# A row softmax on one core: exponentials in a register loop, broadcasting multiplications, one transfer queue

## The chip, the cores and the metric

The kernel runs on one core of a Trainium2 chip. Four of the core's engines matter here: VectorE (DVE in the profile), ScalarE (ACT), GpSimd (POOL) and SyncE (SP). SP computes nothing; it issues transfers. Transfers between the memory off the chip (DRAM in the names, HBM in the profile) and the core's own memory run on 16 DMA engines. They are issued from an engine's instruction queue: a transfer issued by SP goes into SP's data queue (q1 in the profile), one issued by ScalarE into ScalarE's (q10). Engines run on their own and meet at semaphores.

The metric is the device time of one execution in microseconds (us); less is better. The time before is 161.78 us, the median of three runs (161.41 to 161.79).

## What is computed

```python
def reference(x):                      # x: 16 x 1024 x 512, float32
    x_max = np.max(x, axis=-1, keepdims=True)
    exp_x = np.exp(x - x_max)
    return exp_x / np.sum(exp_x, axis=-1, keepdims=True)
```

These are 16,384 rows of 512 numbers. Each row takes a maximum, an exponential of every element less that maximum, the sum of the exponentials, and a multiplication by the sum's reciprocal. 33.55 MB go in and 33.55 MB come out.

## The kernel before

The rows are cut into eight chunks (`CHUNKS`). A chunk gives each of the 128 partitions 16 rows (`CHUNK`), 4.19 MB in all, and is one load (L71) and one store (L74). Its work is done in two groups of eight rows per partition (`GROUP`), so there are 16 groups. The core's memory has places for six chunks (`PLACES`, the tile `held`); results are written over the inputs. So six loads can be issued at once, and loads 6 and 7 go into the places of chunks 0 and 1 once those are stored. `LOAD_AFTER` puts them behind the stores 0 and 1 in the program.

One group takes these steps:

- `rowmax` (L88): one VectorE reduction over 8 x 512 elements of each partition gives eight negated maxima (`shift`).
- `exps` (L93): eight ScalarE instructions of 512 elements each. Each takes one maximum as bias and also accumulates the sum of its row (`sums`). In the profile each shows as an ACTIVATE and a read of the accumulator.
- `scale` (L104, L106): one VectorE reciprocal of the eight sums, then eight multiplications, each of one row by one number per partition.

VectorE does the maximum of group g and then the scaling of group g-1, so that ScalarE has a group to work on meanwhile. All loads are issued from SP's queue and all stores from ScalarE's. A store stands in ScalarE's instruction stream between exponentials; `STORE_BEHIND` says how many groups late. Tile, the framework, keeps the order in which the program is written and adds the semaphores. `loads_at_the_head` moves SP's first load in front of the barrier at the start of the program. The instructions of all loops are written out one by one: the loops in the source are Python's.

Of the kernel before, what the change touches and what calls it, by code (L numbers as in the profile page):

```python
# [1 line left out]

# [4 lines left out]

F32 = mybir.dt.float32
EXP = mybir.ActivationFunctionType.Exp
AX = mybir.AxisListType.X  # L10


CHUNK = 16
CHUNKS = 8
PLACES = 6
GROUP = 8

STORE_BEHIND = [1, 1, 1, 1, 0, 0, 0, 0]

LOAD_AFTER = {0: 6, 1: 7}  # L20


AT_HEAD = {mybir.EngineType.SP: 1}

def loads_at_the_head(nc):

    main, body = nc.main_func.blocks[0], nc.main_func.blocks[1]
    for engine, count in AT_HEAD.items():  # L30
        loads = [
            i
            for i in body.instructions
            if i.engine == engine and type(i).__name__ == "InstDMACopy"
        ][:count]
        barrier = next(
            n
            for n, i in enumerate(main.instructions)
            if i.engine == engine and type(i).__name__ == "InstDrain"
        )  # L40
        for load in loads:
            body.instructions.remove(load)
        main.instructions[barrier:barrier] = loads


@with_exitstack
def kernel(
    ctx: ExitStack,
    tc: tile.TileContext,
    x: bass.AP,  # L50
    out: bass.AP,
):
    nc = tc.nc
    nc.at_finalize(loads_at_the_head)
    P = nc.NUM_PARTITIONS

    x_rows = x.flatten_outer_dims().rearrange("(c p r) d -> c p r d", p=P, r=CHUNK)
    out_rows = out.flatten_outer_dims().rearrange("(c p r) d -> c p r d", p=P, r=CHUNK)
    n, _, _, d = x_rows.shape
    assert n == CHUNKS  # L60

    data = ctx.enter_context(tc.tile_pool(name="data", bufs=1))
    stats = ctx.enter_context(tc.tile_pool(name="stats", bufs=6))
    held = data.tile([P, PLACES * CHUNK, d], F32, name="held")

    def place(k):
        at = (k % PLACES) * CHUNK
        return held[:, at : at + CHUNK, :]

    def load(k):  # L70
        nc.sync.dma_start(out=place(k), in_=x_rows[k])  # L71

    def store(k):
        nc.scalar.dma_start(out=out_rows[k], in_=place(k))  # L74
        if k in LOAD_AFTER:
            load(LOAD_AFTER[k])

    per = CHUNK // GROUP
    groups = CHUNKS * per
    shift, sums = [None] * groups, [None] * groups  # L80

    def rows(g):
        at = (g % per) * GROUP
        return place(g // per)[:, at : at + GROUP, :]

    def rowmax(g):
        shift[g] = stats.tile([P, GROUP], F32, name="shift", tag="shift")
        nc.vector.reduce_max(out=shift[g], in_=rows(g), axis=AX, negate=True)  # L88

    def exps(g):  # L90
        sums[g] = stats.tile([P, GROUP], F32, name="sums", tag="sums")
        for r in range(GROUP):
            nc.scalar.activation(  # L93
                out=rows(g)[:, r, :],
                in_=rows(g)[:, r, :],
                func=EXP,
                bias=shift[g][:, r : r + 1],
                scale=1.0,
                accum_out=sums[g][:, r : r + 1],
            )  # L100

    def scale(g):
        recip = stats.tile([P, GROUP], F32, name="recip", tag="recip")
        nc.vector.reciprocal(out=recip, in_=sums[g])  # L104
        for r in range(GROUP):
            nc.vector.tensor_scalar_mul(  # L106
                out=rows(g)[:, r, :],
                in0=rows(g)[:, r, :],
                scalar1=recip[:, r : r + 1],
            )  # L110

    with tc.manual_schedule():
        for k in range(PLACES):
            load(k)
        stored = 0
        for g in range(groups):
            rowmax(g)
            exps(g)
            if g:
                scale(g - 1)  # L120
            if stored < CHUNKS and g > (stored + 1) * per - 1 + STORE_BEHIND[stored]:
                store(stored)
                stored += 1
        scale(groups - 1)
        while stored < CHUNKS:
            store(stored)
            stored += 1


# [1 line left out]
_INS = ['x']  # L131
_OUTS = [((16, 1024, 512), 'float32')]


# [23 lines left out]
```

## Time and profile before

| | |
|---|---|
| median of three runs | 161.78 us |
| the profiled execution | 161.69 us |
| its span, first to last instruction | 159.9 us |
| VectorE busy | 123.5 us, 77% |
| ScalarE busy | 93.2 us, 58% |
| GpSimd busy | 0.2 us |
| moved | 67.13 MB, mean 420 GB/s |
| a load, issue to landing (median) | 35.4 us |
| a store, issue to landing (median) | 28.4 us |

The profile comes from one execution. The span leaves out 1.8 us of the execution's time. Busy time of an engine counts its computing instructions; issuing a transfer is not counted. The DMA share is the mean busy share of the 16 DMA engines. A queue marked "q" behind an engine's name (SPq, ACTq) is the engine's instruction stream itself, where transfers are issued. A group of instructions is given by line, engine, operation, output <- input, shape and count, then its busy time, the mean of one in ns, and the idle time of the engine just before it with what ended that.

### The profile page before, as it was taken

What the parts mean: (1) busy time and instruction counts of PE and PEld (TensorE: products, weight loads), DVE (VectorE), ACT (ScalarE), POOL (GpSimd) and SP (SyncE); (2) the same over time, 40 slices, a digit from 0 to 9 for tenths busy, and PEclk for the clock granted to TensorE, in tenths of its full rate; (3) what the DMA queues carried; (4) which work ended last, traced back from release to release, by engine and by line L of the source; (5) the groups of instructions that cost most, each with busy time, mean ns of one, the idle gap of its engine ahead of it and who ended that gap; (6) DMA issues with size and microseconds to landing.
All of it is one profiled execution on the core that took longest, in us unless ns stands there. A gap on an engine that the chain in (4) does not pass through costs nothing.

```text
span 159.9 us, 496 instructions
## 1 busy us (share of the span) xinstructions
DVE 123.5 (77%) x160; ACT 93.2 (58%) x257; POOL 0.2 (0%) x4
## 2 busy tenths in 40 slices
DVE  0008969999999999999999999999999997620000
ACT  0003799495959585867777685959594959300000
POOL 0000000000000000000000000000000000000000
DMA  8999999999999999999999999999999999999993
GB/s 270 459 443 402 451 459 402 426 469 410 402 393 393 500 412 402 467 434 410 426 459 410 418 484 404 402 500 410 402 426 484 393 410 500 402 402 500 410 402 148
DMA packets 2307, 67.13 MB, mean 420 GB/s; under 512 B 256, under 2 KB 256, under 8 KB 256
## 3 DMA queue, kind: packets, MB, share of 16 engines
q1 hardware_dynamic: 1152, 33.55, 49.5%
q10 hardware_dynamic: 1152, 33.55, 48.6%
q14 instruction: 3, 0.02, 0.0%
HBM read 33.55 MB, written 33.55 MB: 420 GB/s over the span
## 4 chain that ended last, share of the span: by engine, by line
DMA 48%; DVE 32%; ACT 8%; issue 1%; DVEq 0%; SPq 0%; ACTq 0%
DMA held<-in_x_dram 30%; DVE shift L88 19%; DMA out_dram<-held 18%; DVE held L106 12%; ACT held L93 8%; DVE recip L104 1%; DVEq L153 0%; SPq L71 0%; ACTq L93 0%
## 5 line engine op out<-in xcount | busy, mean ns | idle before, releaser
L93 ACT ACTIVATE held<-held,shift 128x512 f32<-128x512 f32 x128 | 90.5, 708 | 31.5 <-DVE shift L88 21.3
L88 DVE TENSOR_REDUCE shift<-held 128x8 f32<-128x4096 f32 x16 | 70.5, 4415 | 12.7 <-DMA held<-in_x_dram 12.7
L106 DVE TENSOR_SCALAR held<-held,recip 128x512 f32<-128x512 f32 x128 | 52.1, 482 | 0.6
L93 ACT ACTIVATION_READ_ACCUMULATOR held<-held,shift 128x1 f32 x128 | 23.9, 187 | 0.0
L93 ACT ACT_TABLE_LOAD x1 | 1.3, 1283 | 12.6 <-DMA held<-in_x_dram 12.6
L104 DVE RECIPROCAL recip<-sums 128x8 f32<-128x8 f32 x16 | 3.1, 196 | 4.0 <-ACT held L93 4.0
L142 POOL MEMSET const-bfloat16-1.0<- 128x1 bf16 x1 | 0.1, 101 | 0.0
L142 POOL MEMSET const-uint8-127<- 128x1 uint8 x1 | 0.1, 101 | 0.0
L142 POOL MEMSET const-float32-0.0<- 128x1 f32 x1 | 0.1, 98 | 0.2 <-issue 0.2
L142 POOL MEMSET const-float32-1.0<- 128x1 f32 x1 | 0.1, 98 | 0.0
## 6 DMA issues: line engine op xcount, KB each, us to landing
held<-in_x_dram SPq DMA_DIRECT2D x8, 4096.0 KB, 35.4
out_dram<-held ACTq DMA_DIRECT2D x8, 4096.0 KB, 28.4
```

The costliest lines, as they stand in the source:

```text
L88: nc.vector.reduce_max(out=shift[g], in_=rows(g), axis=AX, negate=True)
L93: nc.scalar.activation(out=rows(g)[:, r, :], in_=rows(g)[:, r, :], func=EXP, bias=shift[g][:, r : r + 1], scale=1.0, accum_out=sums[g][:, ...
L104: nc.vector.reciprocal(out=recip, in_=sums[g])
L106: nc.vector.tensor_scalar_mul(out=rows(g)[:, r, :], in0=rows(g)[:, r, :], scalar1=recip[:, r : r + 1],)
L142: nc = _bacc.Bacc("TRN2", target_bir_lowering=False, num_devices=1)
```

## The change

The kernel no longer uses Tile's pools and semaphores for most of its work, but its own semaphores inside sections that Tile treats as one piece (`tile_critical`).

- **Transfers.** There are nine loads and nine stores of one or two groups (`SIZES`); group 0 has a buffer of its own (`first`), the fifteen others go round a ring of eleven groups (`ring`). All are issued by SP, in a fixed order: loads 0 to 6, then `ORDER`, then store 0. SP waits before a store until VectorE and GpSimd have scaled all groups up to it, and before loads 7 and 8 until stores 1 and 2 have landed. Load 0 is still moved to the head.
- **ScalarE.** Group 0's exponentials are written out. The other fifteen groups run in a hardware loop (`Fori`) whose body holds eight exponentials; their addresses come from registers, worked out from the loop counter modulo the ring's size. Each turn waits for a semaphore that VectorE raises for each group of maxima, and lowers it by one. The sum is written over the maximum in the same column (`stat`). The exponential's table is loaded ahead of time.
- **VectorE.** Maxima of chunks 3, 4 and 5 take both groups in one instruction (`WHOLE`). Scaling is two groups behind (`BEHIND`). It is one `tensor_mul` of 8 x 512 elements, whose second operand is the eight reciprocals, each repeated 512 times by its access pattern.
- **GpSimd.** It does the `tensor_mul` of groups 2, 4, 6, 8, 10 and 12 (`ON_POOL`). VectorE still does their reciprocals.
- **Group 0** is scaled and stored last.

The diff, without empty lines:

```diff
@@ -8,16 +8,40 @@
 F32 = mybir.dt.float32
 EXP = mybir.ActivationFunctionType.Exp
 AX = mybir.AxisListType.X
-CHUNK = 16
-CHUNKS = 8
-PLACES = 6
+ACT, DVE, POOL, PE, SP = [
+    getattr(mybir.EngineType, e) for e in ("Activation", "DVE", "Pool", "PE", "SP")
+]
 GROUP = 8
-STORE_BEHIND = [1, 1, 1, 1, 0, 0, 0, 0]
-LOAD_AFTER = {0: 6, 1: 7}
+SIZES = [1, 2, 2, 2, 2, 2, 1, 2, 2]
+CHUNKS = len(SIZES)
+RING = 11
+STARTS = [sum(SIZES[:k]) for k in range(CHUNKS)]
+GROUPS = sum(SIZES)
+BEFORE = {7: 1, 8: 2}
+ORDER = [
+    ("store", 1),
+    ("store", 2),
+    ("load", 7),
+    ("store", 3),
+    ("load", 8),
+    ("store", 4),
+    ("store", 5),
+    ("store", 6),
+    ("store", 7),
+    ("store", 8),
+]
+ON_POOL = [2, 4, 6, 8, 10, 12]
+BEHIND = 2
+WHOLE = (3, 4, 5)
 AT_HEAD = {mybir.EngineType.SP: 1}
@@ -54,77 +78,145 @@
     nc.at_finalize(loads_at_the_head)
     P = nc.NUM_PARTITIONS
-    x_rows = x.flatten_outer_dims().rearrange("(c p r) d -> c p r d", p=P, r=CHUNK)
-    out_rows = out.flatten_outer_dims().rearrange("(c p r) d -> c p r d", p=P, r=CHUNK)
-    n, _, _, d = x_rows.shape
-    assert n == CHUNKS
-    data = ctx.enter_context(tc.tile_pool(name="data", bufs=1))
-    stats = ctx.enter_context(tc.tile_pool(name="stats", bufs=6))
-    held = data.tile([P, PLACES * CHUNK, d], F32, name="held")
-    def place(k):
-        at = (k % PLACES) * CHUNK
-        return held[:, at : at + CHUNK, :]
+    x_rows, out_rows = x.flatten_outer_dims(), out.flatten_outer_dims()
+    d = x_rows.shape[1]
+    assert x_rows.shape[0] == P * GROUPS * GROUP
+    first = ctx.enter_context(nc.sbuf_tensor("first", [P, GROUP * d], F32))
+    ring = ctx.enter_context(nc.sbuf_tensor("ring", [P, RING * GROUP * d], F32))
+    def columns(name, n):
+        return ctx.enter_context(nc.sbuf_tensor(name, [P, n], F32))
+    first_stat, first_recip = columns("first_stat", GROUP), columns("first_recip", GROUP)
+    stat, recip = columns("stat", RING * GROUP), columns("recip", RING * GROUP)
+    def sem(name):
+        return ctx.enter_context(nc.semaphore(name))
+    maxima, summed, inverted, by_vector, by_pool = [
+        sem(s) for s in ("maxima", "summed", "inverted", "by_vector", "by_pool")
+    ]
+    loaded = {k: sem(f"loaded{k}") for k in range(CHUNKS)}
+    stored = {k: sem(f"stored{k}") for k in BEFORE.values()}
+    others = sem("others")
+    def at(g):
+        return (g - 1) % RING
+    def rows(g, groups=1):
+        if g == 0:
+            part = first[:, :]
+        else:
+            part = ring[:, at(g) * GROUP * d : (at(g) + groups) * GROUP * d]
+        return part.rearrange("p (r d) -> p r d", d=d)
+    def cols(t, g, groups=1):
+        return t[:, at(g) * GROUP : (at(g) + groups) * GROUP]
+    def in_dram(t, k):
+        part = t[P * GROUP * STARTS[k] : P * GROUP * (STARTS[k] + SIZES[k]), :]
+        return part.rearrange("(p r) d -> p r d", p=P)
     def load(k):
-        nc.sync.dma_start(out=place(k), in_=x_rows[k])
+        return nc.sync.dma_start(
+            out=rows(STARTS[k], SIZES[k]), in_=in_dram(x_rows, k)
+        )
     def store(k):
-        nc.scalar.dma_start(out=out_rows[k], in_=place(k))
-        if k in LOAD_AFTER:
-            load(LOAD_AFTER[k])
-    per = CHUNK // GROUP
-    groups = CHUNKS * per
-    shift, sums = [None] * groups, [None] * groups
-    def rows(g):
-        at = (g % per) * GROUP
-        return place(g // per)[:, at : at + GROUP, :]
-    def rowmax(g):
-        shift[g] = stats.tile([P, GROUP], F32, name="shift", tag="shift")
-        nc.vector.reduce_max(out=shift[g], in_=rows(g), axis=AX, negate=True)
-    def exps(g):
-        sums[g] = stats.tile([P, GROUP], F32, name="sums", tag="sums")
+        return nc.sync.dma_start(
+            out=in_dram(out_rows, k), in_=rows(STARTS[k], SIZES[k])
+        )
+    def exp(row, one):
+        return nc.scalar.activation(
+            out=row, in_=row, func=EXP, bias=one, scale=1.0, accum_out=one
+        )
+    def spread(t):
+        return t.unsqueeze(2).to_broadcast([P, GROUP, d])
+    def rowmax(g, groups):
+        k = max(c for c in range(CHUNKS) if STARTS[c] <= g)
+        nc.vector.wait_ge(loaded[k], 16)
+        nc.vector.reduce_max(
+            out=cols(stat, g, groups), in_=rows(g, groups), axis=AX, negate=True
+        ).then_inc(maxima, groups)
+    def exps():
+        with nc.Fori(0, GROUPS - 1, 1, engines=(ACT,)) as g:
+            nc.scalar.wait_ge(maxima, 1).then_inc(maxima, -1)
+            row = nc.scalar.snap((g % RING) * GROUP)
+            for r in range(GROUP):
+                done = exp(ring[:, bass.ds((row + r) * d, d)], stat[:, bass.ds(row + r, 1)])
+            done.then_inc(summed, 1)
+    def scale(g):
+        nc.vector.wait_ge(summed, g)
+        nc.vector.reciprocal(out=cols(recip, g), in_=cols(stat, g)).then_inc(inverted, 1)
+        engine, scaled = nc.vector, by_vector
+        if g in ON_POOL:
+            engine, scaled = nc.gpsimd, by_pool
+        engine.wait_ge(inverted, g)
+        engine.tensor_mul(
+            out=rows(g), in0=rows(g), in1=spread(cols(recip, g))
+        ).then_inc(scaled, 1)
+    def store_scaled(k):
+        groups = STARTS[k] + SIZES[k] - 1
+        on_pool = sum(g <= groups for g in ON_POOL)
+        nc.sync.wait_ge(by_vector, groups - on_pool)
+        if on_pool:
+            nc.sync.wait_ge(by_pool, on_pool)
+        store(k).then_inc(stored.get(k, others), 16)
+    with tc.manual_schedule(engines={ACT, DVE, POOL, SP}):
+        head = load(0)
+        head.then_inc(loaded[0], 16)
+        tc.info.no_tile_sem_insts.add(head.ins.name)
+        nc.scalar.preload_act_table(EXP)
+        with tc.tile_critical(sync_engine=SP):
+            for k in range(1, min(BEFORE)):
+                load(k).then_inc(loaded[k], 16)
+        nc.vector.wait_ge(loaded[0], 16)
+        behind = [
+            nc.vector.reduce_max(
+                out=first_stat[:], in_=rows(0), axis=AX, negate=True
+            )
+        ]
         for r in range(GROUP):
-            nc.scalar.activation(
-                out=rows(g)[:, r, :],
-                in_=rows(g)[:, r, :],
-                func=EXP,
-                bias=shift[g][:, r : r + 1],
-                scale=1.0,
-                accum_out=sums[g][:, r : r + 1],
-            )
-    def scale(g):
-        recip = stats.tile([P, GROUP], F32, name="recip", tag="recip")
-        nc.vector.reciprocal(out=recip, in_=sums[g])
-        for r in range(GROUP):
-            nc.vector.tensor_scalar_mul(
-                out=rows(g)[:, r, :],
-                in0=rows(g)[:, r, :],
-                scalar1=recip[:, r : r + 1],
-            )
-    with tc.manual_schedule():
-        for k in range(PLACES):
-            load(k)
-        stored = 0
-        for g in range(groups):
-            rowmax(g)
-            exps(g)
-            if g:
-                scale(g - 1)
-            if stored < CHUNKS and g > (stored + 1) * per - 1 + STORE_BEHIND[stored]:
-                store(stored)
-                stored += 1
-        scale(groups - 1)
-        while stored < CHUNKS:
-            store(stored)
-            stored += 1
+            behind.append(exp(rows(0)[:, r, :], first_stat[:, r : r + 1]))
+        with tc.tile_critical(sync_engine=PE):
+            exps()
+            seen = 1
+            for g in range(1, GROUPS):
+                if g == seen:
+                    k = max(c for c in range(CHUNKS) if STARTS[c] <= g)
+                    take = SIZES[k] if k in WHOLE else 1
+                    rowmax(g, take)
+                    seen += take
+                if g > BEHIND:
+                    scale(g - BEHIND)
+            for g in range(GROUPS - BEHIND, GROUPS):
+                scale(g)
+            for what, k in ORDER:
+                if what == "store":
+                    store_scaled(k)
+                else:
+                    nc.sync.wait_ge(stored[BEFORE[k]], 16)
+                    load(k).then_inc(loaded[k], 16)
+        nc.vector.reciprocal(out=first_recip[:], in_=first_stat[:])
+        behind.append(
+            nc.vector.tensor_mul(out=rows(0), in0=rows(0), in1=spread(first_recip[:]))
+        )
+        behind.append(store(0))
+        for one in behind:
+            tc.declare_no_dep(one.ins, head.ins, reason="VectorE waits for loaded[0]")
+        with tc.tile_critical(sync_engine=SP):
+            nc.sync.wait_ge(others, 16 * (CHUNKS - 1 - len(stored)))
 # ---- launch: one core; inputs and outputs as the reference has them ----
```

## The prediction

> **What bounds the kernel now.** I read the page's busy shares first, then the slices of the span, the queues, the chain that ended last, and windows by stage. Busy shares and slices (the rows are VectorE, ScalarE, GpSimd, DMA share and GB/s, each in 40 slices of 4 us):
>
> ```profile
> span 159.9 us, 496 instructions
> DVE 123.5 (77%) x160; ACT 93.2 (58%) x257; POOL 0.2 (0%) x4
> DVE  0008969999999999999999999999999997620000
> ACT  0003799495959585867777685959594959300000
> DMA  8999999999999999999999999999999999999993
> ```
>
> VectorE (DVE) is full in the middle, but has nothing to do for the last 19 us, and DMA is full from the second slice to the last but one. The queues and the instruction groups (mean ns follows the busy time):
>
> ```profile
> q1 hardware_dynamic: 1152, 33.55, 49.5%
> q10 hardware_dynamic: 1152, 33.55, 48.6%
> q14 instruction: 3, 0.02, 0.0%
> ...
> L93 ACT ACTIVATE held<-held,shift 128x512 f32<-128x512 f32 x128 | 90.5, 708 | 31.5 <-DVE shift L88 21.3
> L88 DVE TENSOR_REDUCE shift<-held 128x8 f32<-128x4096 f32 x16 | 70.5, 4415 | 12.7 <-DMA held<-in_x_dram 12.7
> L106 DVE TENSOR_SCALAR held<-held,recip 128x512 f32<-128x512 f32 x128 | 52.1, 482 | 0.6
> ```
>
> The two data queues together keep the DMA engines at work for 98.1% of the span: all but 3.0 us. So 67.1 MB of traffic set the time. The chain of waits begins with the first load (0.00 to 12.48) and later runs through DMA twice; its VectorE pieces decide only when transfers are issued, not when they end. Windows by stage (busy time of each engine, TensorE clock, DMA share, GB/s) for start, loads alone, both queues, stores alone, end:
>
> ```profile
> 0.00:4.00 4.00, 0.00 (x0) 0.00 (x0) 0.20 (x4) 1.00 0.81 270
> 4.00:39.80 35.80, 25.70 (x27) 19.89 (x54) 0.00 (x0) 1.00 1.01 437
> 41.00:119.00 78.00, 77.65 (x102) 58.12 (x163) 0.00 (x0) 1.00 1.01 430
> 120.00:156.00 36.00, 18.16 (x29) 12.95 (x37) 0.00 (x0) 1.00 0.99 429
> 156.00:159.90 3.90, 0.00 (x0) 0.00 (x0) 0.00 (x0) 1.00 0.35 151
> ```
>
> Nowhere is there a hole in the middle to win back. A faster kernel can only gain from the rate and the two ends; a slower one needs a moment when the queue runs empty.
>
> **The change, part by part.** The profiled execution took 161.69 us: a span of 159.9 and 1.8 around it. The median of the runs is 161.78, so 0.1 is added at the end. I call 8 rows of every partition a group (2.097 MB; 16 of them), as the kernel does.
>
> *Transfers.* Same bytes, one queue. The first 4.19 MB landed at 12.48; one more load to issue in the same time (SP's first six issues took 3.2 us together) fits beside load 0's 4.8 us. The remaining 62.9 MB, by the slowest row (429) take 146.7 us, by the fastest (437) 143.9. The completion records of one DMA engine, which have no window edges, lie between: 9.68 us from load to load while loads ran alone (11.24, 20.92, 30.60, 40.28) and again 9.68 from store to store at the end (128.23, 137.91, 147.59, 157.27), or 433 GB/s. These are stages in which one queue ran alone, which is what the changed kernel has throughout, so I take 433: 145.2 us. 12.5 + 145.2 = 157.7 for the last landing, where before has 140.77 + 18.3 (the last store's issue and its time to landing) = 159.1. The 1.4 us are what before loses where the second queue starts (packets of about 1.9 us instead of 1.21 at 42.8, and a window of 416 GB/s from 41 to 60) and where it fetches instructions (three times, q14). The second goes if ScalarE's 257 instructions become a loop. Four of the 18 transfers are half as large, in pieces of 16 KB: 0.1 us, a guess between 0 and 0.3. Sum: 157.7 + 0.1 + 0.8 (end of the last landing to end of the span) + 1.8 = 160.4; with the median's 0.1, 160.5. With 437 it is 159.1, with 429 161.9.
>
> A skill page speaks against this term: the Trainium skill, "DMA: Bandwidth & Descriptors", Issuing engines are not separate DMA queues, says that transfers of all issuers share the same engines and that the issuer changes only issue time. By it the queue's change would be worth nothing and only the fetches would go, which leaves about 161.3.
>
> *Does compute keep the one queue fed?* SP now waits in order, so a late store holds up all behind it. With 4.85 us per group (half of 9.7) and 12.48 for the first two, the queue has brought the seven loads ahead of the loop (12 groups) at 61.0, then ends store 1 at 70.7, 2 at 80.4, load 7 at 90.1, store 3 at 99.8, load 8 at 109.5, stores 4 to 8 at 119.2, 128.9, 133.7, 143.4, 153.1, store 0 at 158. A store has to be issued before the one ahead of it is done, by a lead of 1 us (issue at 0.00, bytes in the second microsecond) to 3.8 us (the first store, issued 39.88, shows its first packet at 43.65), and 1 us more since landings trail the data. So store 1 by 56 to 59, store 5 by 114 to 117, store 7 by 129 to 132, store 8 by 138 to 141, store 0 by 148 to 151. Loads 7 and 8 wait for stores 1 and 2, but stores 2 and 3 lie ahead of them in the queue as 9.7 us of cover each.
>
> *VectorE.* Per group it drops eight TENSOR_SCALAR (3.26 us, from the timeline) for one broadcasting multiplication of 4096 elements. Not in the trace; at the least the 3.26 that it replaces, at the most two passes of the reduce's 4.42 (8.8). I take 4.4: the reduce is the nearest row, 4096 elements in one instruction. Six of the sixteen go to GpSimd (POOL): unknown too, from one reduce's 4.4 to two passes, 8.8. Whether the two engines' multiplications can overlap is also unknown; I walk the worst of it, 8.8 and no overlap. Load 0 lands at 7.6; maximum to 12.0; exponentials of group 0 to 17.7 (8 x 0.705, the pitch of ACTIVATE). Maxima 1 and 2 to 26.2, 3 (landed 27.0) to 31.4, multiplication 1 to 36.0, maximum 4 to 40.4, then GpSimd's multiplication 2, 40.7 to 49.5, beside a double maximum of the same 8.8. From there VectorE repeats 13.6 us per two groups (double maximum 8.8, multiplication 4.4, two reciprocals 0.4) and GpSimd fits in: 4 done at 63, 6 at 77, 8 at 90. Behind that the maxima are single, so multiplications 9, 11 and 13 wait 4.4 each for GpSimd: 10 done at 108, 11 at 112.5, 12 at 126, 13 at 130, 14 and 15 at 135 and 139.5, group 0 at 144.5. Every store is in time, 7 and 8 just so (130 against 129 to 132, 139.5 against 138 to 141): cost 0 to 1.6 us. If the two engines overlap, or GpSimd takes 4.4, all of the end is 8 us earlier and costs 0. I take 0.
>
> One rule makes this tighter. The Trainium skill, "GPSIMD Engine Reference", Elementwise — side-by-side cycle accounting, has 4497 ns for a two-input operation of 2048 elements, so an estimate of 8.9 to 9.0 for 4096, and "SBUF — State Buffer", SBUF: two separate sides, has such operations exclude a two-input VectorE operation; no run here shows either. By these pages the sum would have 0.2 to 2 us of empty queue and lie at 160.7 to 162.5.
>
> *ScalarE.* The loop adds to every exponential the arithmetic for two addresses, and to every group a wait, a decrement and a branch. Low bound 0: the queue works ahead of the engine, as the store issued between exponentials shows (below, 0.38 us on the queue and the pitch stays 0.70). High bound: that row for each address, 2 x 0.34, of which 0.38 hides: 0.3 per exponential, 2.4 per group. The semaphore events of that queue took 17 ns, and register work is nearer to these: I take 0. ScalarE needs 5.65 us per group and has up to 7.5: first loop exponential at 21.8, last due before 15's multiplication at 135.
>
> ```profile
> 39.76 0.71 ACT L93 ACTIVATE held<-held,shift 128x512 f32<-128x512 f32 x1
> 39.88 0.38 ACTq L74 DMA_DIRECT2D out_dram<-held  x1
> 40.37 0.19 ACT L93 ACTIVATION_READ_ACCUMULATOR held<-held,shift 128x1 f32 x1
> 40.46 0.71 ACT L93 ACTIVATE held<-held,shift 128x512 f32<-128x512 f32 x1
> ```
>
> The hand-made critical sections add meetings of the engines at their ends, at the 0.2 to 0.6 us that SP waited for such signals; the slack of group 0's store covers it. The early table load (1.28 us) was hidden before by the first maximum.
>
> **Rivals.** *A, slower: the multiplications exclude each other and GpSimd's takes over 9 us.* Six of them then form a chain with VectorE's, and each microsecond above 9 costs 6: at 10 us, 166. For it: VectorE is already the fullest engine (77%). Against: at 9 or less nothing runs empty.
> *B, slower: ScalarE's loop takes over 7.5 us per group.* The fifteen groups are serial, so each microsecond above costs about 15: at 8 us, some 166; at the high bound (8.05), 167. Against it: the store's issue above.
> *C: the one queue gains nothing.* Turning from loads to stores within a queue, five times, costs what the second queue's start cost (0.7 a packet), so 3.5: 164; with half of it 162. Against: with both queues at work the engines alternate all along at 430 GB/s.
>
> **How the numbers follow.** Forecast 0.60, own range 159.1 to 161.9; A 0.13 (161 to 168), B 0.12 (162 to 175), C 0.15 (161 to 164). About 0.3%, 0.5 us, is what a measurement can tell: faster is below 161.3, slower above 162.3. The forecast gives 0.55 faster, 0.05 same; C 0.03, 0.05, 0.07; A 0.01, 0.02, 0.10; B 0.12 slower. Together 0.59, 0.12, 0.29. The range goes from 159.3 to 165.5, leaving out the ends of A and B and a little below.
>
> **What would show it.** Right: one data queue near 98% of a shorter span, a last landing near 157.7, no instruction fetch, DMA share 0.97 or more from 12 to 150, pitch of exponentials 0.70 to 0.75. A shows as VectorE multiplications with idle time until GpSimd ends and a dip in DMA after 130; B as a pitch over 0.9; C as dips near 61, 80, 90, 100 and 110. The prediction falls if any stage in the middle has a DMA share under 0.9.

## The result and the profile after

The changed kernel is slower, by half a per cent: 162.39 us (median of 20 runs, 161.6 to 163.21) against 161.61 for the kernel before in the same comparison; the ratio is 1.0046, 95% interval 1.0026 to 1.0066. The profiled execution took 162.86 us with a span of 161.1.

The page's busy shares and slices after (VectorE, ScalarE, GpSimd, DMA share in 40 slices), and the data queues:

```profile
span 161.1 us, 611 instructions
...
DVE 122.9 (76%) x39; ACT 92.5 (57%) x257; POOL 42.3 (26%) x10
...
DMA  7999999999999999999999999999999999999990
...
q1 hardware_dynamic: 2592, 67.11, 97.5%
```

All transfers are in one queue, no instruction is fetched (there is no q14 line), and DMA is full from the second slice to the last but one. The same windows by stage as before, with the end of the span as one more (busy time of each engine, TensorE clock, DMA share, GB/s):

```profile
0.00:4.00 4.00, 0.00 (x0) 1.28 (x1) 0.20 (x4) 1.00 0.79 233
4.00:39.80 35.80, 25.95 (x7) 22.74 (x64) 0.00 (x0) 1.00 1.02 439
41.00:119.00 78.00, 73.87 (x23) 59.62 (x169) 37.70 (x6) 1.00 1.00 431
120.00:156.00 36.00, 20.84 (x9) 7.43 (x22) 2.89 (x1) 1.00 0.99 429
156.00:159.90 3.90, 0.00 (x0) 0.00 (x0) 0.00 (x0) 1.00 0.35 151
159.90:161.10 1.20, 0.00 (x0) 0.00 (x0) 0.00 (x0) 1.00 0.00 0
```

These rows hardly differ from those of before: 439, 431 and 429 GB/s against 437, 430 and 429. The middle has no hole and no gain. The last row is the difference that can be seen here: 1.2 us without a byte.

The engines' own work went as the walk in the prediction had it, or better. Groups of instructions (busy time and mean ns of one, then idle time before):

```profile
L134 ACT ACTIVATE ring<-ring,stat x120 | 84.8, 709 | 24.2 <-ACTq L151 24.2
...
L164 POOL TENSOR_TENSOR ring<-ring,recip 128x4096 f32<-128x4096 f32 x6 | 42.1, 7016 | 80.4 <-DVE recip L159 80.4
L164 DVE TENSOR_TENSOR ring<-ring,recip 128x4096 f32<-128x4096 f32 x9 | 47.4, 5266 | 0.3
...
L213 DVE TENSOR_TENSOR first<-first,first_recip 128x4096 f32<-128x4096 f32 x1 | 4.4, 4424 | 0.0
```

A broadcasting multiplication takes VectorE 4.42 us when alone and GpSimd 7.02. VectorE's mean is higher (5.27), and the timeline shows why: VectorE's of 84.54 begins beside GpSimd's of 80.19 and ends 4.3 us after GpSimd's end at 87.21.

```profile
80.19 7.02 POOL L164 TENSOR_TENSOR ring<-ring,recip 128x4096 f32<-128x4096 f32 x1 [6.22 <-DVE recip L159]
```

```profile
80.03 4.37 DVE L145 TENSOR_REDUCE stat<-ring 128x8 f32<-128x4096 f32 x1
84.31 0.19 DVE L159 RECIPROCAL recip<-stat 128x8 f32<-128x8 f32 x1
84.54 6.95 DVE L164 TENSOR_TENSOR ring<-ring,recip 128x4096 f32<-128x4096 f32 x1
```

So the two engines' multiplications do exclude each other, while a maximum (80.03, 4.37 us) runs beside GpSimd undisturbed. It cost nothing here: the last store was issued at 141.25.

What the windows average away is in the trace's completion records: each of the 16 DMA engines leaves one, a packet of 4 bytes, when it has done its part of a transfer. The trace does not name the engines, so the table gives the earliest and the latest of the sixteen records of each transfer, in us; they need not be the same engines all along. Below, "the first engine" and "the last engine" mean these two:

```
changed kernel            first engine   last engine   apart
load 5 done                   55.03         55.65       0.62
load 6 done                   60.44         61.30       0.86
store 2 done                  79.81         80.66       0.86
load 7 done                   89.49         90.81       1.32
store 3 done                  99.17        100.49       1.32
load 8 done                  108.85        110.90       2.05
store 0 done (the end)       157.30        159.34       2.05
```

Load 6 is one group: 4.84 us at the pace of the others, but 5.41 passed at the first engine, 5.65 at the last and 5.22 in the mean of the sixteen. After that the first engine keeps 9.68 us per transfer of two groups. The last one does too, except in loads 7 and 8, the two that are followed by a store: it loses 0.47 and 0.72 us more there. I call such a place a turn, from loads to stores within the queue. The kernel before ended with its engines 1.50 apart, at 157.27 and 158.77: the first engine gained nothing from the change, and the last lost 0.57.

From the last completion to the end of the span 1.72 us passed, 1.14 before. After SP has seen the last landing (159.70), it goes through the closing section: a branch, the wait for the other stores, a drain and the meeting with the framework's semaphores, 0.56 us one behind the other. Then comes what the kernel before does too. With 0.57 at the last engine and 0.58 here the difference of 1.2 us between these two spans is complete. The profiled execution (162.86) is one of the longer ones of its kernel; the medians differ by 0.8 us.

### The profile page after: what moved, and what is told of

The parts are those of the page before. It is cut to its first block, busy times and chain, and to the rows that moved or that the text cites. A ratio compares the mean times of both kernels' runs of the same rounds, so it can differ in the third digit from the quotient of the medians.

```text
span 161.1 us, 611 instructions
## 1 busy us (share of the span) xinstructions
DVE 122.9 (76%) x39; ACT 92.5 (57%) x257; POOL 42.3 (26%) x10
## 4 chain that ended last, share of the span: by engine, by line
DMA 47%; DVE 30%; issue 5%; POOL 4%; SPq 0%; DVEq 0%
DMA ring<-in_x_dram 35%; DVE stat L145 14%; DMA out_dram<-ring 13%; DVE ring L164 13%; POOL ring L164 4%; DVE first L213 3%; DVE recip L159 1%; SPq L124 0%; DVE first_recip L211 0%; DVEq L192 0%; SPq L245 0%; DVEq L211 0%; SPq L173 0%; SPq L181 0%
## 5 line engine op out<-in xcount | busy, mean ns | idle before, releaser
L134 ACT ACTIVATE ring<-ring,stat x120 | 84.8, 709 | 24.2 <-ACTq L151 24.2
L145 DVE TENSOR_REDUCE stat<-ring 128x8 f32<-128x4096 f32 (+1 forms) x12 | 65.4, 5457 | 10.2 <-ACT first L134 6.0
L164 POOL TENSOR_TENSOR ring<-ring,recip 128x4096 f32<-128x4096 f32 x6 | 42.1, 7016 | 80.4 <-DVE recip L159 80.4
L164 DVE TENSOR_TENSOR ring<-ring,recip 128x4096 f32<-128x4096 f32 x9 | 47.4, 5266 | 0.3
L134 ACT ACTIVATION_READ_ACCUMULATOR ring<-ring,stat x120 | 22.6, 188 | 0.0
L134 ACT ACTIVATE first<-first,first_stat 128x512 f32<-128x512 f32 x8 | 5.7, 708 | 10.0 <-DVE first_stat L186 10.0
L186 DVE TENSOR_REDUCE first_stat<-first 128x8 f32<-128x4096 f32 x1 | 4.4, 4420 | 7.6 <-DMA first<-in_x_dram 7.6
L213 DVE TENSOR_TENSOR first<-first,first_recip 128x4096 f32<-128x4096 f32 x1 | 4.4, 4424 | 0.0
L159 DVE RECIPROCAL recip<-stat 128x8 f32<-128x8 f32 x15 | 2.9, 192 | 0.0
L134 ACT ACTIVATION_READ_ACCUMULATOR first<-first,first_stat 128x1 f32 x8 | 1.5, 187 | 0.0
```

Source lines behind the costliest of these rows:

```text
L134: return nc.scalar.activation(out=row, in_=row, func=EXP, bias=one, scale=1.0, accum_out=one)
L145: nc.vector.reduce_max(out=cols(stat, g, groups), in_=rows(g, groups), axis=AX, negate=True).then_inc(maxima, groups)
L159: nc.vector.reciprocal(out=cols(recip, g), in_=cols(stat, g)).then_inc(inverted, 1)
L164: engine.tensor_mul(out=rows(g), in0=rows(g), in1=spread(cols(recip, g))).then_inc(scaled, 1)
L186: nc.vector.reduce_max(out=first_stat[:], in_=rows(0), axis=AX, negate=True)
L213: nc.vector.tensor_mul(out=rows(0), in0=rows(0), in1=spread(first_recip[:]))
```

## The experiments

The theory after the result, T: the transfers alone set the time; the first store costs all engines about half a microsecond, whichever queue it is in; each later turn costs the engines that are behind; and the closing section costs its length. Its first rival, R: computing disturbs the transfers, or a store comes too late.

**Transfers alone.** The first kernel leaves all computing out: SP waits for the load where it waited for the scaling.

```diff
-                if what == "store":
-                    store_scaled(k)
+                if what == "store":
+                    nc.sync.wait_ge(loaded[k], 16)
+                    store(k).then_inc(stored.get(k, others), 16)
```

> All computing is left out: every store waits for its own load alone, so the output is the input and not the softmax. Transfers, their sizes, their order, the one queue and the closing section are those of the changed kernel. Theory T (the turns from loads to stores and the closing section cost the time, compute costs nothing): last landing within 0.5 us of the changed kernel's, the last DMA engine at 158.5 to 159.5, time 162.0 to 163.0; the loss of about 0.57 us before the first store's packets is there again. Rival R (computing disturbs the transfers, or a store comes late): at least 0.7 us less than the changed kernel, 161.5 or below.

Measured: 162.71 us, ratio to before 1.0056 (1.0036 to 1.0076), the changed kernel's ratio within the intervals. The completion records are almost the same: load 6 done at 60.35 to 61.26, load 7 at 89.41 to 90.80, load 8 at 108.77 to 110.89, the end at 157.22 to 159.34. R falls: the same 18 transfers in this order take this time without any computing.

The second has the stores in ScalarE's queue (`nc.scalar.dma_start`, and ScalarE waits for `loaded[k + 2]` up to store 4).

> As the copy with one queue, computing left out and output not the softmax, but stores are issued by ScalarE, store k of 1 to 4 once load k+2 has landed. T: no later turn from loads to stores within a queue, so the DMA engines stay closer together and the last one ends 0.3 to 0.8 us earlier: 161.3 to 162.2. If the queue makes no difference: within 0.2 us of the copy with one queue. If the start of a second queue costs, as the prediction had it: 0.7 to 1.1 us more than with one queue.

Measured: 162.15, ratio 1.0014 (0.9989 to 1.0039). That is 0.4% less than in one queue, by intervals that just overlap; the profiled execution shows the engines 1.8 apart at the end instead of 2.1. It is as T had it in time, weakly, and it isn't what the prediction had: the second queue costs no 0.7 us.

**The kernel before with one queue.** This is the prediction's term by itself.

```diff
-LOAD_AFTER = {0: 6, 1: 7}
+LOAD_AFTER = {1: 6, 2: 7}
...
-        nc.scalar.dma_start(out=out_rows[k], in_=place(k))
+        nc.sync.dma_start(out=out_rows[k], in_=place(k))
```

> The kernel before with the one edit that all transfers are in SP's queue, loads 6 and 7 one store later. The prediction's term (one queue alone runs at 433 GB/s and saves the second queue's start): 0.7 to 1.1 us less than before, about 160.7. T: the first turn costs the same 0.6 us whichever queue the store is in, and two more turns cost up to 0.7: 161.6 to 162.3, no gain. Instruction fetches stay three in both.

Measured: 163.06, ratio 1.0063 (1.0043 to 1.0082): with one queue, and loads 6 and 7 one store later, the kernel before is 1 us slower. The three fetches are still there, one data queue now:

```profile
q1 hardware_dynamic: 2304, 67.11, 97.6%
q14 instruction: 3, 0.02, 0.0%
```

There is a loss ahead of the first store here too: the transfer before it takes the first engine 10.31 us (50.18 to 60.49) instead of 9.68. At the two later turns the last engine falls behind by 0.35 and 1.34 us, and the end is at 157.40 to 160.05. The gain that I predicted is a loss, larger than the upper end of T's figure.

Turns alone do not account for this loss. One packet follows the other on each engine, so the last engine can be followed back through the trace: it is the one that did the fetches at 34.48 and 104.25. Each took 0.31 us, and the packet behind it was 0.33 and 0.25 us longer than the others, so 0.56 of the 1.34 us are the second fetch. The other fifteen engines are done by 158.62, where the kernel before ends at 158.77. So one queue gains nothing, and the loss of 1 us was measured together with fetches; what one queue costs this kernel without them no run shows.

**One turn fewer.** Loads 7 and 8 go one behind the other.

```diff
     ("load", 7),
-    ("store", 3),
     ("load", 8),
+    ("store", 3),
     ("store", 4),
```

> The changed kernel with loads 7 and 8 one behind the other, then stores 3 and 4, which takes away one of three turns from loads to stores. T: the spread between the first and the last DMA engine at the end is 1.2 to 1.7 instead of 2.0 us, time 0.2 to 0.7 us less than the changed kernel. If turns cost nothing: the same within 0.2 us.

Measured: 161.82, ratio 0.999 (0.9973 to 1.0007), and the range of the runs shrinks to 161.66 to 162.32. The engines end 157.32 to 158.15, 0.83 apart instead of 2.05 (1.2 to 1.7 was expected). Two entries of the order exchanged take back all that the change lost. The times show this, not the two profiles: the one here is of the shortest of twelve executions, that of the changed kernel of a long one. The lag differs between executions of one order: the kernel with its closing section on ScalarE (below) has the changed kernel's order, and in the profile of its shortest execution the engines end 1.12 apart.

**Turns counted.** Sixteen loads and stores of one group, transfers alone; the two kernels differ in the order of issue, stores and loads by turns or in two rows.

> Transfers alone in one queue (computing left out, output is the input), all sixteen groups a transfer each, five turns from loads to stores. T: each turn behind the first costs the slowest DMA engine about 0.4 us: spread between first and last engine at the end 2.2 to 3.0 us, 0.8 to 1.6 us more than with two turns. If a turn costs nothing: the same as with two turns within 0.3 us.

> The same sixteen loads and sixteen stores, issued in an order with two turns from loads to stores. T: spread at the end 0.9 to 1.4 us. If a turn costs nothing: the same time as with five turns.

Measured: 163.64, ratio 1.0111 (1.0085 to 1.0137), with five turns, and 162.03, ratio 1.0015 (0.9995 to 1.0036), with two. Three turns cost 1.6 us, the upper end of what was expected. In the profiled executions the engines end 1.87 and 0.81 apart, both less than expected, and the first engine 157.98 and 157.82: most of it is again the late engines' loss. The engine that is last before a turn is the one that loses most there in most cases: over these runs, with 0.7 to 1.0 us of lag it loses 0.1 to 0.5, with 1.2 to 1.5 us of lag 0.2 to 0.8, leaving out transfers that a fetch falls into. The packets that grow are an engine's last loads, at a time when the others are at the first store. Why such a load takes longer, no run shows.

**The first store, early.** In the two-turn kernel, store 1 goes behind load 4.

```diff
-            for k in range(1, min(BEFORE)):
+            for k in range(1, 5):
+                load(k).then_inc(loaded[k], 16)
+            nc.sync.wait_ge(loaded[1], 16)
+            store(1).then_inc(stored[1], 16)
+            for k in range(5, min(BEFORE)):
                 load(k).then_inc(loaded[k], 16)
```

> Transfers alone (computing left out, output is the input), as the copy with two turns, but store 1 is issued behind load 4, so the first turn from loads to stores comes at about 27 us and there are three in all. If all 16 engines lose 0.3 to 0.6 us at the very first store, whenever it comes: that loss is at 27 and the turn at about 60 costs the first engine 0.1 or less. If it belongs to a long row of loads: the loss of 0.3 to 0.6 is again at 60.

Measured: 162.91, ratio 1.006 (1.0039 to 1.0081), with three turns. Load 4, ahead of the first store, takes the first engine 5.37 us instead of 4.86, a loss of 0.51 at 27 us; the turn that was the first one now comes at 66 us and costs that engine 0.03. So the loss comes with the first store, wherever it stands. Its size is not fixed: in the two-turn kernel, whose first store comes at about 60 us, load 11 ahead of it took the first engine 5.17 us, and in the mean of the sixteen the loss there was only 0.09, after 0.02 to 0.04 in each of the six loads before it. With five turns it was 0.06, in the changed kernel 0.36, in the kernel before with one queue 0.78. What sets it, no run shows.

Two more kernels tried to hide it behind the start with a small write at the head: 16 rows of 512 B from input to output, from ScalarE's queue. One is the version with loads 7 and 8 together and the closing section on ScalarE (below), the other the kernel before.

```diff
-AT_HEAD = {mybir.EngineType.SP: 1}
+AT_HEAD = {mybir.EngineType.SP: 1, mybir.EngineType.Activation: 1}
...
+        early = nc.scalar.dma_start(out=out_rows[0:16, 0:128], in_=x_rows[0:16, 0:128])
```

> The version with two loads together and the closing section on ScalarE, and one more transfer: 16 rows of 512 B copied from the input to the output at the head, from ScalarE's queue; store 0 writes over them at the end. If the loss of 0.3 to 0.6 us on all engines belongs to the first write to HBM: it goes from 55 to 60 us and hides behind the first packets, 0.2 to 0.5 us less than the same program without the write. If it belongs to the first large store after a row of loads: no difference, or 0.1 more.

> The kernel before with the same small write to HBM at the head from ScalarE's queue. If the slow packets of all 16 engines at 42.8 us belong to the first write to HBM or to the start of the second queue: they go, 0.3 to 0.6 us less than before, ratio 0.996 to 0.998. If they belong to the first large store: they stay at about 43 us, ratio 0.999 to 1.002.

Measured: 163.3, ratio 1.0096 (1.0072 to 1.012), against 0.9982 without the write; and 162.04, ratio 1.0006 (0.9987 to 1.0025). In the first, the framework made the other loads wait for that write, and the queue was empty for 1.5 us about 7 us into the span, which is the loss in time; the first store's loss is still there (load 6 takes 5.60 us at the first engine). In the second, the slow packets of the engines are still at 41 to 44 us, although the queue of ScalarE had been used at the head. So it is neither the first write to HBM nor the start of a queue that costs this. The small write differed from the first store in two ways: it came out of HBM, and it moved 8 KB. Whether the loss goes with the first store out of the core's memory or with the first large one, no run separates.

**The closing section** moves to ScalarE, where it runs before the last landing.

```diff
-        with tc.tile_critical(sync_engine=SP):
-            nc.sync.wait_ge(others, 16 * (CHUNKS - 1 - len(stored)))
+        with tc.tile_critical(sync_engine=ACT):
+            nc.scalar.wait_ge(others, 16 * (CHUNKS - 1 - len(stored)))
```

> The changed kernel with its closing section (the wait for the other stores) on ScalarE, where it is over before the last store lands, instead of behind that landing on SP. Theory T: from the last DMA engine's end to the end of the span 1.1 to 1.2 us as before instead of 1.7, so 0.4 to 0.6 us less than the changed kernel, ratio to before about 1.001 to 1.002. Rival (that section runs beside the landing's notice and costs nothing): no difference, ratio 1.004 to 1.006.

Measured: 162.21, ratio 1.0025 (1.0002 to 1.0049). Last completion to end of span is 1.17 us instead of 1.72; the times give 0.3 us, less than the 0.4 to 0.6 expected and with intervals that overlap. With loads 7 and 8 together as well:

> Both edits: loads 7 and 8 one behind the other, closing section on ScalarE. T: the two savings add: 161.1 to 161.5, ratio to before 0.994 to 0.997, faster than both kernels. If either was chance: ratio 0.998 to 1.002.

> The same program as two_loads_end_on_act, for comparison on the same chip: ratio to before 0.996 to 1.0.

Measured: 161.65, ratio 0.9984 (0.9958 to 1.0009), and in the second sample 161.43, ratio 0.9982 (0.9966 to 0.9997). This version is 0.6% faster than the changed kernel and 0.2% faster than the one before; only the second sample excludes no difference. The two savings do not simply add, as T had it (0.994 to 0.997): the times lie where the expectation put them if one of the savings was chance, and beyond the exchange of the loads (0.999) they give the closing section only 0.1 us, within the noise. By the times its saving is not shown; that the section lies behind the last landing is what the profiles show (1.17 us from the last completion to the end here, 1.73 with the loads exchanged alone). The page, of the second sample:

```profile
span 159.6 us, 612 instructions
...
q1 hardware_dynamic: 2592, 67.11, 98.5%
q14 instruction: 1, 0.01, 0.0%
```

The section on ScalarE brings one fetch back, at 157.70, when the first engine was already done.

**The compute parts undone.** With ScalarE's loop written out:

```diff
-        with nc.Fori(0, GROUPS - 1, 1, engines=(ACT,)) as g:
-            nc.scalar.wait_ge(maxima, 1).then_inc(maxima, -1)
-            row = nc.scalar.snap((g % RING) * GROUP)
+        for g in range(GROUPS - 1):
+            nc.scalar.wait_ge(maxima, g + 1)
+            row = (g % RING) * GROUP
```

> The changed kernel with ScalarE's loop written out (addresses and waits constant), nothing else. Instruction fetches come back. The prediction's term (the three fetches cost the DMA engines that do them about 0.4 us of the 1.4): 0.3 to 0.5 us more than the changed kernel. Theory T: a fetch is one 8 KB packet of 0.31 us on one engine and only counts where that engine is the last anyway: 0 to 0.4 us more, the ratio to before 1.003 to 1.008. If register addresses hold up ScalarE: a shorter pitch of the exponentials than the loop's 0.705 us and less time.

Measured: 163.99, ratio 1.0128 (1.0103 to 1.0153). The loop is a part that gains, and much more than I had given it: 1.3 us. Two fetches are back:

```profile
span 162.3 us, 415 instructions
...
q1 hardware_dynamic: 2592, 67.11, 96.8%
q14 instruction: 2, 0.02, 0.0%
```

The records of fetches are 0.31 us each, at 31.18 and 84.35, and the engine behind them ends last: its packets right after are 0.32 and 0.29 longer, and at the turns it loses 1.10 and 0.71, so that the end is at 157.33 to 160.62. That looked as if turns multiplied what a fetch delays. The test was the same with loads 7 and 8 together (both edits above):

> ScalarE's loop written out, so two instruction fetches, and loads 7 and 8 one behind the other, so one later turn from loads to stores instead of two. If a fetch costs so much because the engine that it delays loses more at each turn: most of the 1.3 us that writing out the loop cost goes, ratio to before 1.001 to 1.006, spread of the DMA engines at the end 1.2 to 2.0 us instead of 3.3. If a fetch costs 0.6 us each anywhere: the two savings just add, ratio 1.006 to 1.009 (1.0128 less the 0.0056 of the turn).

Measured: 163.67, ratio 1.0106 (1.008 to 1.0132), more than either case. Against the same order with the loop (0.999) writing it out costs 1.2%, 1.9 us. Here it isn't one late engine alone: nearly all lose 0.1 to 0.3 us around 80 and 0.2 to 0.8 around 97, where the looped kernel lost next to nothing. The losses around 80 come before the second fetch, at 84.75. So writing the loop out, which brings back two fetches of 0.31 us, costs 1.3 to 1.9 us. That the fetches cause all of it is not shown, and how stays open; multiplication at the turns is part of the picture in one profiled execution and not the whole.

With the multiplications as before, VectorE alone, row by row:

```diff
-ON_POOL = [2, 4, 6, 8, 10, 12]
+ON_POOL = []
...
+        for r in range(GROUP):
+            done = nc.vector.tensor_scalar_mul(
+                out=rows(g)[:, r, :],
...
```

> The changed kernel with the multiplications as before: VectorE alone, eight row by row per group, GpSimd idle. Working for a group takes VectorE 4.42 + 0.2 + 3.26 = 7.9 us, group 15 would be scaled at about 136, every store in time. T: the same time as the changed kernel within 0.3 us, so the broadcasting multiplications and GpSimd's share gain and lose nothing. Rival (GpSimd's work slows something on the path): 0.5 us less or more.

Measured: 162.89, ratio 1.0069 (1.0048 to 1.009), 0.4 us above the changed kernel (0.3 was expected at most) with intervals that overlap. VectorE's program is long enough for one fetch (q14 shows one), so I don't ascribe that difference to the multiplications. A gain of the broadcasting ones beyond that fetch is not shown.

With the broadcasting ones all on VectorE, only the first of these two edits:

> The changed kernel with all broadcasting multiplications on VectorE, none on GpSimd. VectorE needs 4.42 + 0.2 + 4.42 = 9.04 us per group: fifteen groups from 18.0 end at 153.6, store 7 is about 12 us late and the queue runs empty there: 170 to 175, ratio 1.05 to 1.08. If another bound held: the changed kernel's time.

Measured: 171.97, ratio 1.0628 (1.0595 to 1.0661), as walked. Windows of that kernel (VectorE, ScalarE, GpSimd busy, clock, DMA share, GB/s):

```profile
100.00:123.00 23.00, 22.90 (x9) 14.63 (x43) 0.00 (x0) 1.00 1.01 433
...
133.00:156.00 23.00, 22.66 (x10) 8.10 (x24) 0.00 (x0) 1.00 0.59 254
```

Here the queue does run empty: VectorE is full, and DMA is at 0.59 where store 7 waits. This is how a compute bound would have looked, and the changed kernel shows none of it. GpSimd's six groups are needed, but only because the multiplication was made slower for VectorE (4.42 instead of 3.26 us) in the same change.

## Why the prediction was wrong

It forecast 160.5 us, faster; it came out at 162.39, slower, above the forecast's own range (159.1 to 161.9). By its steps:

- *What bounds the kernel* was right: the transfers alone reproduce the time.
- *"One queue alone ... so I take 433: 145.2 us"* is the step that failed. I took the pace of single stages, in which only loads or only stores run, and put them end to end. The pace holds (9.68 us per 4.19 MB all along), but not the seams. In the profiled execution SP saw the last landing at 159.70 instead of 157.8 (the 157.7 with 0.1 for the smaller pieces). The 1.9 us are the first store, 0.57, and the last engine's extra loss at the first turn, 0.24, at the second, 0.47, and at the third, 0.72 (2.0 in all).
- *"What before loses where the second queue starts"* was a misreading of the cause, so one queue did not win it back. The slow packets at 42.8 us are the first store's: a loss stands ahead of the first store in one queue too, at 60 us or at 27. Whether a second queue adds to it is open. The mean of the sixteen engines was about 0.6 us with two queues, in the kernel before and in the copy, and 0.1 to 0.8 with one.
- *Rival C* was the right one, at 0.15: "with half of it 162". Its count was off: three turns lead from loads to stores, and the two from stores to loads cost little. The cost of a later turn is on the engines that are behind, not on all. That its 162 lies so near is in part luck.
- *The instruction fetches* were mis-sized, as far as the loop's worth is theirs: I gave all three together a part of 1.4 us; writing the loop out, with two fetches, costs 1.3 to 1.9. That they would go was right.
- *"The slack of group 0's store covers"* the sections was wrong for the closing one, which lies behind the last landing: 1.37 us from there to the end of the span instead of 0.8.
- *Compute keeps the queue fed*: right, with more room than thought. GpSimd took 7.02 us, between the bounds of 4.4 and 8.8, and VectorE 4.42, as taken. Exclusion, the worse case, holds. Rival A needed over 9 us and had no occasion.
- *ScalarE's loop costs nothing*: right. Rival B falls: the pitch of 0.70 to 0.71 us holds also from one turn of the loop to the next, as the last exponential of a group (27.76) and the first of the next (28.46) show:

```profile
27.76 0.71 ACT L134 ACTIVATE ring<-ring,stat  x1
28.37 0.19 ACT L134 ACTIVATION_READ_ACCUMULATOR ring<-ring,stat  x1
28.46 0.71 ACT L134 ACTIVATE ring<-ring,stat  x1
```

- *The skill's pages.* The Trainium skill, "DMA: Bandwidth & Descriptors", Issuing engines are not separate DMA queues, was nearer to the truth than my term, in that it gives the queue no gain. But the kernel before with one queue is 0.63% slower, and the copy with one queue takes 1.0056 against 1.0014 with two, so the queue need not be indifferent. That this is because it fixes the order in which loads and stores meet is my reading, not shown by these two pairs. "SBUF — State Buffer", SBUF: two separate sides, is confirmed in its exclusion by 6.95 us instead of 4.42. The estimate of 8.9 to 9.0 us from "GPSIMD Engine Reference", Elementwise — side-by-side cycle accounting, was too high for this multiplication, whose second operand is broadcast: 7.02.

Put together, the change is a sum of opposite parts: the loop is worth about 1.3 us, one queue costs about 1.0 (with fetches), the closing section about 0.5 by the profile. They come to 0.2 us, not to the 0.8 us measured. The parts were measured in different surroundings (the loop in the changed kernel, the queue in the one before), and the remaining 0.6 us isn't ascribed. What is shown with separate intervals is the order: without one of its three turns the changed kernel loses nothing.

## What to carry to other kernels

Where transfers set the time, look at the order in which loads and stores follow each other in a queue, not only at whether the queue is full: a DMA share near 1.0 hid 2 us here, and putting two loads together was worth 0.6%. See whether what must wait at the end can go to an engine whose wait is over before the last store lands, and read a cost at the end of the span from the records behind the last landing. Before you credit a cost to the part that stands beside it, as I did with the second queue, ask what else happened there for the first time. And before you credit an order or a queue with a loss, see which engine ends last and what else it did: in the kernel before with one queue it was the one that fetched instructions.

## What the runs showed of the hardware that I had not expected

- Ahead of the first large store out of the core's memory the DMA engines lose time, at 27, 42 or 60 us and in either queue: 0.06 to 0.78 us in the mean of the sixteen, by kernel. A small copy from HBM to HBM ahead of it doesn't take it away.
- DMA engines that are behind lose more at most later turns from loads to stores within one queue (up to 0.8 us at one turn, where no fetch falls into the transfer). After the last turn the distance stays to the hundredth (2.05 us from load 8 to the end in the changed kernel).
- Writing ScalarE's loop out, which brings two instruction fetches of 0.31 us, costs this kernel, bound by transfers, 1.3 to 1.9 us. In the kernel before with one queue, the engine that did two fetches ends 1.4 us after the other fifteen.
- Register addresses, a wait and a branch in ScalarE's loop cost nothing beside exponentials of 0.705 us.
